# Five scheduling changes at once in a two-layer hybrid decoder: order of weight splits, table work, warm-up fillers, mixing

## The chip, the core and the metric

The kernel runs on one core of one Trainium2 chip. A core has five engines that each follow a list of instructions in order and meet at semaphores: TensorE (PE, matrix products into PSUM), VectorE (DVE), ScalarE (ACT), GpSimd (POOL) and SyncE (SP, which here only issues DMAs). The metric is the device time of one execution in microseconds. Half a per cent is about 2.5 us here.

## The reference

For 512 tokens of width 1024 the reference runs two layers, all in float32. Each layer computes

```
h = rmsnorm(x, norm_g);  p = h @ w_in        # split by columns into four head groups
A: latent attention, 4 heads: q = rmsnorm(rmsnorm(cq) @ w_uq), rotated in 32 of 96 columns;
   k from rmsnorm(ckv) @ w_ukv and one rotated key for all heads; causal softmax, times v
B: c_b * short_conv(c_c * c_h)               # width 3 along the tokens
C: sg_u * (tril(sg_w) @ layernorm(sg_v) + sg_b)   # inside chunks of 128 tokens
D: block-sparse attention on mq, mk, mv, rotated in 16 of 64 columns
x = x + concat(A*silu(g_a), B*silu(g_b), C*silu(g_c), D*silu(g_d)) @ w_out
```

## The kernel before, in words

**Tiles.** The tokens are four tiles t of 128 rows. For each, `pre_norm` (L632) forms `h` on DVE (x times the row's reciprocal norm times the gain `ng`), PE transposes it (`hT`), and ACT and DVE split it into a high part `hTh` and a low part `hTl`. A float32 product is made of three products of such parts by `mm3` (L260): high by high, high by low, low by high. Every weight is split in the same way.

**Units.** A weight block is a `Unit`: SP loads it into one of two `raw` slots, ACT (or DVE, where its planned clock is ahead) writes `whi`, DVE writes `wlo` (`split_units`, L395; for the first four units POOL writes the second low half), and PE uses both. There are six `whi`/`wlo` slots. The units stand in one list, `order`; `unit()` (L437) marks the next `AHEAD` units of the list as wanted when one is used, and an unwanted unit is only split while ACT and DVE are idle by plan.

**The planner.** Nothing of the order is left to a scheduler of the compiler. `Order` (L69) runs when the program is built: chains of work are generators with a due time and a priority, and four clocks (A, V, G, D for ACT, DVE, POOL and DMA) and `now` (PE's time) follow planned costs. Whatever chain comes next writes its instruction, and so fixes the order on its engine. All instructions of `_emit` carry L164 and those of `pe()` L194, so the profile tells them apart by tile names. If PE is idle by plan before 15 us, `pe()` writes fillers. On the chip the engines keep this order, and wait where the plan was too early.

**Around the change.** `start()` (L1548) writes the beginning: the load of the gain row `gz` on ACT's DMA queue, products of ones (`warm`), the transpose of the positions, and `ng`, a product that copies the gain row to all partitions. `rope_tables()` (L481) computes sine and cosine for the rotations with some 50 small operations on DVE, or on POOL when DVE is not free. `load_params` and `mix_chain` (L837) prepare and issue the mixing of group C: `sgw` is masked and split, the chain waits for the four tiles of `vn` (the normed `sg_v`, split into `vnh` and `vnl`), takes an `h` slot for `mix`, and writes the products `mp`. `mla_heads` (L1169) starts attention A with the transposes `t0a` of Q and `t1a` of K; it waits for all tiles of Q and K and their rotation. The output product runs as seven half-size products (`ZPROD`), whose results lie in PSUM banks of two pools (accS and sS).

**Order in each layer.** `cq` (the latent columns), then `sq` (`sg_v` and `mq`, four units), `ga`, `mp`, `kv`, attention A, the other feature columns, attention D, and the output product.

Of the kernel before, what the change touches and what calls it, by code (L numbers as in the profile page):

```python
# [18 lines left out]
P = 128  # L19
# [11 lines left out]

NRAW, NW, NT2 = 2, 6, 9
WSLACK = 0.0
AHEAD = 4
NWARM, FILL, FILLEND = 3, 0.6, 15000.0
ROPET, PAUSE, MIXT = 3900.0, (4700.0, 15500.0), 23000.0
LOPOOL = (("c0_0", 1), ("c1_0", 1), ("c2_0", 1), ("c3_0", 1))
LOPRIO = -5
ROPEB, ROPEV = 400.0, 200.0
EARLY = ('sq0', 'sq1', 'sq2')  # L40
YORDER, YCUT = (2, 3, 0, 1, 4, 6, 5, 7), 6
# [27 lines left out]
class Order:  # L69
# [20 lines left out]
    def resume(self, prio, gen):  # L90
        try:
            w = next(gen)
        except StopIteration:
            return
        if isinstance(w, Event):
            if w.t is None:
                w.waiters.append((prio, gen))
            else:
                self.spawn(gen, self.now, prio)
        else:  # L100
            self.spawn(gen, w, prio)
# [51 lines left out]
class Chain:  # L153
# [30 lines left out]
    def pe(self, cost, f, *a, **k):  # L184
        if self.t != self.pe_t:
            while self.t + PEMARGIN > self.o.now:
                yield self.t + PEMARGIN
        if self.o.now < self.o.fill_until:
            for _ in range(int((self.o.now - self.o.pe_end) * FILL / 110.0)):
                self.o.fill()  # L190
        self.o.now += cost
        self.o.pe_end = self.o.now
        self.t = self.pe_t = self.o.now + PELAT
        f(*a, **k)  # L194
# [12 lines left out]
def hybrid_trunk(ctx: ExitStack, tc: tile.TileContext, x, positions, norm_g, w_c, w_f, w_t, w_o, mla_q_norm_g,  # L207
# [27 lines left out]
    v4S = Slots(o, 4, lambda name, shape, dt: v4p.tile(shape, dt, tag="v4", name=name))  # L235
    ydS = Slots(o, 2, lambda name, shape, dt: big.tile(shape, dt, tag="yd", bufs=2, name=name))
    tkS = Slots(o, 2, lambda name, d: tkp.tile([P, NT, 4, d], F32, tag="tk", name=name))
    hS = Slots(o, 2, lambda name: wk.tile([P, D], F32, tag="h", bufs=2, name=name))
    yaS = Slots(o, 1, lambda name: wk.tile([P, S], F32, tag="ya", name=name))
    obS = Slots(o, 1, lambda name: wk.tile([P, S], F32, tag="ob", name=name))  # L240
    zzS = Slots(o, 1, lambda name: wk.tile([P, S + 2], F32, tag="zz", name=name))
# [33 lines left out]

    x1d = dr.tile([S, D], F32, name="x1d")


    class Unit:
        def __init__(self, src, a, b, name):  # L280
            self.src, self.a, self.b, self.name = src, a, b, name
            self.loaded, self.ready, self.wanted = Event(), Event(), False
            self.half, self.landed = [Event(), Event()], [Event(), Event()]
            self.slots = eS if name[:-2] in EARLY else wS

        def view(self):
            n = self.a * self.b
            return (self.hi[:, :n].rearrange("p (a b) -> p a b", a=self.a),
                    self.lo[:, :n].rearrange("p (a b) -> p a b", a=self.a))

    units, order = {}, []
    early = []

    def early_make(name):
# [100 lines left out]
    def split_units(i0, i1):  # L395
        for u in order[i0:i1]:
            ch = Chain(o)
            if u.name != "c0_0":
                yield from ch.wait(u.loaded)
            u.hi, u.lo = yield from u.slots.get(ch, u.name)  # L400
            n = u.a * u.b
            for i in range(2):
                if u.name == "c0_0":
                    yield from ch.wait(u.landed[i])
                while ch.t > o.now + SLACK:
                    yield ch.t - SLACK
                while not u.wanted and max(o.clk["A"], o.clk["V"]) > o.now + WSLACK:
                    yield o.now + 100.0
                sl = slice(i * n // 2, (i + 1) * n // 2)
                c2 = Chain(o, max(o.now, ch.t))  # L410
                hi, lo, raw = u.hi[:, sl], u.lo[:, sl], u.raw[:, sl]
                if o.clk["V"] + 600.0 < o.clk["A"] and u.idx > 3:
                    yield from c2.dve_fast(V.tensor_copy, hi, raw)
                else:
                    yield from c2.act(A.activation, hi, raw, AF.Copy)
                if u.idx < 4:
                    o.spawn(low_half(u, i, c2, lo, raw, hi), None, LOPRIO)
                    continue
                yield from c2.dve(V.tensor_tensor, lo, raw, hi.bitcast(F32), op=ALU.subtract)
            if u.idx < 4:  # L420
                continue
            ch.t = c2.t
            u.raw_slots.put(ch)
            o.set(u.ready, ch.t)

    def low_half(u, i, ch, lo, raw, hi):
        if (u.name, i) in LOPOOL:
# [8 lines left out]

    def unit(ch, name, half=None):  # L437
        u = units[name]
        for v in order[u.idx:u.idx + AHEAD]:
            v.wanted = True  # L440
        yield from ch.wait(u.ready if half is None else u.half[half])
        return u.view()
# [3 lines left out]
    def shared(slots, n):  # L446

        left = [n]

        def put(ch):  # L450
            left[0] -= 1
            if left[0] == 0:
                slots.put(ch)
        return put
# [25 lines left out]

    def rope_tables():  # L481
        ch = Chain(o)
        sc = yield from t2S.get(ch, "rope_scratch")
        def carve(i):
            return sc[:, i * 64:(i + 1) * 64].rearrange("p (t i) -> p t i", t=NT)
# [4 lines left out]

        def free_engine():

            while True:
                if ch.t > o.now + SLACK:
                    yield ch.t - SLACK
                if PAUSE[0] < o.now < PAUSE[1]:
                    yield PAUSE[1]
                if o.clk["V"] <= o.now + ROPEV:
                    return True
                if o.clk["G"] <= o.now + SLACK:  # L500
                    return False
                yield o.now + 60.0
# [90 lines left out]
    for l in range(DEPTH):  # L593
        L = Layer()
        L.l = l
        L.ng_ev = Event()
        L.hT, L.hTh = [[Event(), Event()] for _ in range(NT)], [[Event(), Event()] for _ in range(NT)]
        L.xss = [cst.tile([P, 4], F32, name=f"xss{t}_{l}") for t in range(NT)]
        L.qd = [Event() for _ in range(NT)]
        L.kd = [Event() for _ in range(NT)]  # L600
# [31 lines left out]
    def pre_norm(L, t, xx, t0, release):  # L632
# [4 lines left out]
        yield from ch.wait(L.ng_ev)  # L637
        h = yield from hS.get(ch, f"h{t}_{L.l}")
        hput = shared(hS, 2)
        tps = []  # L640
        for c in range(2):
            sl = slice(c * 512, (c + 1) * 512)
# [194 lines left out]
    def mix_chain(L):  # L837
# [11 lines left out]
        obS.put(ch)  # L849
        for t in range(NT):  # L850
            yield from ch.wait(L.vn_ev[t])
        L.mix = (yield from hS.get(ch, f"mix{l}")).rearrange("p (n g d) -> p n g d", n=NT, g=4)
        for g2 in range(2):
            mp = yield from accS.get(ch, f"mp{g2}_{l}")
# [314 lines left out]
    def mla_heads(L):  # L1169
# [2 lines left out]
            yield from ch0.wait(L.qd[t])  # L1172
            yield from ch0.wait(L.kd[t])
        yield from ch0.wait(L.kr_ev)

        def prep(H):
            H.prep_ev = [Event(), Event()]
            H.op = [None, None]
# [178 lines left out]
    def main():  # L1357
# [24 lines left out]
        def seven(L):  # L1382
# [33 lines left out]

            bank, evs = {}, {}
            home = {"b11": "z", "b21": "z", "t3": "x", "t4": "x"}
            slot = {"z0": accS, "z1": accS, "x0": accS, "x1": sS, "y0": sS, "y1": sS}
            for n in ZPROD:  # L1420
                for i in range(2):
                    b = home.get(n, "y") + str(i)
# [5 lines left out]
                    a = bank[b]  # L1428
                    if (l, n, i) == (DEPTH - 1, "b22", 1):
                        ev2 = Event()  # L1430
                        yield from z_out(L, "u", i, a, m.t, ev2, sS.put)
                        for c0, c1 in TAIL:
                            a = yield from accS.get(m, f"ot{c0}_{l}")
                            yield from prod(n, i, a, True, c0, c1)
                            o.spawn(z_out(L, n, i, a, o.now + PELAT, Event(), accS.put, c0, c1))
                        continue
                    yield from prod(n, i, a, n in ("b11", "t3"))
                    if n == "b11":
                        y = bank[f"y{i}"] = yield from sS.get(m, f"oy{i}_{l}")
                        o.spawn(minus(i, a, y, o.now + PELAT, ev))  # L1440
                    else:
                        o.spawn(z_out(L, n, i, a, o.now + PELAT, ev,
                                      slot[b].put if n in ("b21", "t4", "b22") else None))
# [102 lines left out]
    L0.x0, L0.xh = [Event() for _ in range(NT)], [Event(), Event()]  # L1546

    def start():  # L1548
        o.clk["D"] = 1000.0
        cw = Chain(o)  # L1550
        ones = (yield from zzS.get(cw, "ones"))
        gz = yield from hS.get(cw, "gz")
        nc.scalar.dma_start(gz[0:1, :], dram(norm_g, 0, [[D, 1], [1, D]]))
        yield from cw.dve_fast(V.memset, ones[:, 0:256], 1.0)
        wp = yield from accS.get(cw, "warm")
        for _ in range(NWARM):
            PE.matmul(wp[:, 0:256], ones[:, 0:P], ones[:, 0:256], start=True, stop=True)
        PE.transpose(wp[:, 256:256 + NT], junk[0:NT, P:2 * P], ident[0:NT, 0:NT])
        V.tensor_copy(posf, wp[:, 256:256 + NT])
        L0.ng = []  # L1560
        for c in range(2):
            L0.ng.append((yield from sS.get(cw, f"ng{c}")))
            PE.matmul(L0.ng[c], ones[0:1, 0:P], gz[0:1, c * 512:(c + 1) * 512], start=True, stop=True)
        o.pe_end, o.fill_until = 6300.0, FILLEND
        o.fill = lambda: PE.transpose(wp[:, 0:P], ident, ident)
        o.clk["V"] = 3700.0
        zzS.put(Chain(o, 6000.0))
        hS.put(Chain(o, 6000.0))

        def fill_end():  # L1570
            o.fill_until = 0.0
            accS.put(Chain(o))
            return
            yield
        o.spawn(fill_end(), FILLEND, -9)
        L0.ng_ev.t = 6200.0
        cg = Chain(o)
        x0 = yield from v4S.get(cg, "x0_0", [P, D], F32)
        L0.x[0] = x0
# [15 lines left out]
        o.spawn(load_units(), None, 4)  # L1595
        o.spawn(split_units(0, 4), None, LOPRIO)
        o.spawn(split_units(4, len(order)), None, 5)
        o.spawn(rope_tables(), ROPET, 6)
        o.spawn(main(), None, 10)
        for t in range(NT):  # L1600
            def pre(t):
# [64 lines left out]
```

## Time and profile before

| what | value |
|---|---|
| median of 3 runs (lowest, highest) | 498.72 us (497.2, 499.32) |
| profiled execution | 499.26 us |
| its span | 497.6 us |
| DVE, ACT, POOL busy | 384.1, 320.7, 150.6 us |
| data moved | 81.98 MB, 165 GB/s in the mean |

The span runs from the first to the last recorded instruction; the execution's own time is 1.66 us longer. The ends of PE's matrix products are modelled, so PE's busy time is an upper value, and the starts are the better measure: 512 columns take 0.227 us start to start once the clock is up. In the timelines a row has the start, the length, engine, line, operation, output and inputs, and in brackets the idle time of that engine just before, with what ended it.

### The profile page before, as it was taken

To read this page: it belongs to the slowest core of one execution; us is meant where nothing else is said; L and a number is where in the kernel's file an instruction comes from. 1 tells how busy PE (TensorE), PEld (TensorE's weight loads), DVE (VectorE), ACT (ScalarE), POOL (GpSimd) and SP (SyncE) were. 2 spreads that over 40 slices of the span, in tenths; PEclk is the share of its full clock that TensorE was granted. 3 is DMA by queue.
4 is the path that set the end of the run, shared out by engine and by line. 5 is a ranking of instruction groups with operands and counts; after the bars stand their busy time and mean duration, and the time that the engine had idled before them with its cause. 6 is when DMAs were issued, how large, how long until landed. Compare 5 with 4: busy or idle time off the path is not lost.

```text
span 497.6 us, 7823 instructions
## 1 busy us (share of the span) xinstructions
PE 490.7 (99%) x2459; PEld 416.4 (84%) x2459; DVE 384.1 (77%) x998; ACT 320.7 (64%) x938; POOL 150.6 (30%) x310
## 2 busy tenths in 40 slices
PE   8999989999999999999999999999999999999997
PEld 5998878888888888888889987788888888888886
DVE  3887885567797978699898698757888979765992
ACT  5788754557767786667566995557868676524640
POOL 4656785566100000000041478634250010000000
PEclk9999999999999999999999999999999999999999
DMA  8446549472752445587573232576259464475652
GB/s 306 110 144 212 198 100 235 147 156 54 202 139 84 149 148 135 157 315 247 165 258 129 84 125 88 193 191 102 67 191 232 150 154 122 166 258 180 229 171 96
DMA packets 35459, 81.98 MB, mean 165 GB/s; under 512 B 7125, under 2 KB 16857, under 8 KB 35162
## 3 DMA queue, kind: packets, MB, share of 16 engines
q1 hardware_dynamic: 26960, 73.09, 43.1%
q0 software_dynamic: 8448, 8.39, 11.3%
q8 instruction: 19, 0.31, 0.3%
q14 instruction: 22, 0.18, 0.1%
q10 hardware_dynamic: 10, 0.01, 0.0%
HBM read 73.61 MB, written 24.64 MB: 197 GB/s over the span
## 4 chain that ended last, share of the span: by engine, by line
PE 89%; DVE 3%; ACT 3%; POOL 3%; issue 1%; POOLq 0%; DVEq 0%
PE kv L194 10%; PE cq L194 8%; PE oy L194 6%; PE ch L194 4%; PE cc L194 4%; PE gd L194 4%; PE gb L194 4%; PE cb L194 4%; PE gc L194 4%; PE su L194 4%; PE ox L194 4%; PE oz L194 4%; PE sa L194 3%; PE ga L194 2%; PE od L194 2%; PE oa L194 2%
## 5 line engine op out<-in xcount | busy, mean ns | idle before, releaser
L164 ACT ACTIVATE pd<-pd,mnd 128x256 f32<-128x256 f32 (+3 forms) x48 | 26.0, 555 | 1.4 <-DVE mnd L164 1.4
L164 ACT ACTIVATE pha<-pTa 128x512 fp32r<-128x512 f32 (+3 forms) x32 | 13.9, 436 | 20.0 <-PE pTa L194 19.8
L194 PE MATMUL kv<-whi_kv,hTh 128*128 128x512 f32 x64 | 25.9, 405 | 0.0
L164 ACT ACTIVATE pa<-pa,mna 128x256 f32<-128x256 f32 (+3 forms) x46 | 23.9, 537 | 2.7 <-DVE mna L164 2.7
L164 ACT ACTIVATE phd<-pTd 128x512 fp32r<-128x512 f32 (+3 forms) x32 | 13.8, 434 | 17.8 <-PE pTd L194 17.8
L164 DVE TENSOR_TENSOR pla<-pTa,pha 128x512 fp32r<-128x512 f32 (+3 forms) x32 | 15.2, 484 | 12.8 <-ACT pha L164 12.7
L194 PE MATMUL kv<-whi_kv,hTl 128*128 128x512 f32 x64 | 25.0, 391 | 0.0
L194 PE MATMUL kv<-wlo_kv,hTh 128*128 128x512 f32 x64 | 24.9, 390 | 0.0
L194 PE MATMUL cq<-whi_c,hTh 128*128 128x416 f32 x64 | 24.4, 382 | 0.0
L339 POOL DMA_DIRECT2D t<-in_w_o_dram x16 | 17.5, 1097 | 19.9 <-DMA t<-t 19.3
L194 PE MATMUL cq<-whi_c,hTl 128*128 128x416 f32 x64 | 23.0, 360 | 0.0
L194 PE MATMUL cq<-wlo_c,hTh 128*128 128x416 f32 x64 | 22.9, 357 | 0.0
L164 POOL TENSOR_SCALAR xss<-xss 128x1 f32<-128x1 f32 x8 | 3.1, 391 | 61.8 <-ACT jk L164 49.1
L164 ACT ACTIVATE whi_t<-raw_t 128x512 fp32r<-128x512 f32 x31 | 18.2, 621 | 5.7 <-DMA raw_t<-t 5.7
L164 DVE TENSOR_TENSOR wlo_t<-raw_t,whi_t 128x512 fp32r<-128x512 f32 x32 | 21.1, 683 | 0.0
L164 DVE CUSTOM_DVE_ANT_0 pa<-sa,maskb 128x512 f32<-128x512 f32 (+3 forms) x32 | 15.0, 482 | 6.2 <-PE sa L194 3.1
L164 DVE CUSTOM_DVE_ANT_0 pd<-sd,maskb 128x256 f32<-128x256 f32 (+3 forms) x32 | 14.9, 485 | 5.9 <-PE pTd L194 2.8
L194 PE MATMUL sq<-yTh,hTh 128*128 128x512 f32 x48 | 18.9, 393 | 0.0
L194 PE MATMUL sq<-yTh,hTl 128*128 128x512 f32 x48 | 18.7, 390 | 0.0
L194 PE MATMUL sq<-yTl,hTh 128*128 128x512 f32 x48 | 18.7, 389 | 0.0
L164 DVE TENSOR_TENSOR pld<-pTd,phd 128x512 fp32r<-128x512 f32 (+3 forms) x32 | 15.3, 482 | 3.2 <-ACT phd L164 3.1
L164 ACT ACTIVATE whi_b<-raw_b 128x512 fp32r<-128x512 f32 x24 | 14.5, 622 | 4.2 <-DMA raw_b<-in_w_o_dram 4.2
(379 smaller groups left out, 1856.0 us busy)
## 6 DMA issues: line engine op xcount, KB each, us to landing
t<-in_w_o_dram POOLq DMA_DIRECT2D x16, 512.0 KB, 6.7
raw_t<-t SPq DMA_DIRECT2D x16, 512.0 KB, 4.2
raw_b<-in_w_o_dram SPq DMA_DIRECT2D x12, 512.0 KB, 4.4
raw_sq<-in_w_t_dram SPq DMA_DIRECT2D x8, 512.0 KB, 3.6
t<-in_w_o_dram SPq DMA_DIRECT2D x8, 512.0 KB, 4.4
raw_kv<-in_w_t_dram SPq DMA_DIRECT2D x8, 512.0 KB, 3.5
t<-t SPq DMA_DIRECT2D x8, 512.0 KB, 5.5
ys<-ysc SPq DMA_DIRECT2D x14, 256.0 KB, 4.8
```

The costliest lines, as they stand in the source:

```text
L164: f(*a, **k)
L194: f(*a, **k)
L339: nc.gpsimd.dma_start(z_src(l, n, j), quad(l, b, j), accum_op=ALU.add, max_dma_last_dim=1024)
```

## The change

- Splits: AHEAD goes from 4 to 5. A unit's split gets priority -1 while the unit is one of the next two (URGENT), and 5 otherwise. The fourth unit of `sq` is split into the two `h` slots instead of a weight slot, once the last tile's `h` has its slot.
- Tables: the first 18 operations go to DVE at once; the rest only from 30 us planned time, when DVE or POOL is free. The pause from 4.7 to 15.5 us goes.
- Fillers: products of 128 x 128 ones in place of transposes, one for 215 ns of planned idle time instead of 110. `ng` uses all 128 rows of a `gz` that DVE and POOL zero first; the load of the gain row follows the zeroing.
- Mixing: `mix_chain` goes on 2000 ns of planned time after the last `vn` is ready.
- Output product: three of the six PSUM banks come from the other pool.

```diff
-AHEAD = 4
+AHEAD = 5
-ROPET, PAUSE, MIXT = 3900.0, (4700.0, 15500.0), 23000.0
+ROPET, ROPE0, MIXT = 30000.0, 18, 23000.0
+MIXLAG = 2000.0
+URGENT, PIPE = 2, False
...
-            for _ in range(int((self.o.now - self.o.pe_end) * FILL / 110.0)):
+            for _ in range(int((self.o.now - self.o.pe_end) * FILL / 215.0)):
...
-            self.slots = eS if name[:-2] in EARLY else wS
+            self.slots = eS if name[:-2] in EARLY else HPair(int(name[-1])) if name[:-2] == "sq3" else wS
...
                 while not u.wanted and max(o.clk["A"], o.clk["V"]) > o.now + WSLACK:
                     yield o.now + 100.0
+                if u.idx > 3:
+                    yield o.now, 5 if u.idx > current[0] + URGENT else -1
...
+            done[0] += 1
+            if done[0] <= ROPE0:
+                ch.t = o.now
+                return True
+            if done[0] == ROPE0 + 1:
+                yield ROPET
             while True:
                 if ch.t > o.now + SLACK:
                     yield ch.t - SLACK
-                if PAUSE[0] < o.now < PAUSE[1]:
-                    yield PAUSE[1]
...
         for t in range(NT):
             yield from ch.wait(L.vn_ev[t])
+        yield max(o.now, ch.t) + MIXLAG
...
-            slot = {"z0": accS, "z1": accS, "x0": accS, "x1": sS, "y0": sS, "y1": sS}
+            slot = {"z0": accS, "z1": sS, "x0": sS, "x1": sS, "y0": accS, "y1": accS}
...
+        G.memset(gz[:, 512:1024], 0.0)
+        yield from cw.dve_fast(V.memset, ones[:, 0:256], 1.0)
+        yield from cw.dve_fast(V.memset, gz[:, 0:512], 0.0)
         nc.scalar.dma_start(gz[0:1, :], dram(norm_g, 0, [[D, 1], [1, D]]))
-        yield from cw.dve_fast(V.memset, ones[:, 0:256], 1.0)
         wp = yield from accS.get(cw, "warm")
-        for _ in range(NWARM):
-            PE.matmul(wp[:, 0:256], ones[:, 0:P], ones[:, 0:256], start=True, stop=True)
+        o.clk["V"] = 3000.0
+        def dense(n):
+            PE.matmul(wp[:, 0:n], ones[:, 0:P], ones[:, 0:n], start=True, stop=True)
+        dense(256)
         PE.transpose(wp[:, 256:256 + NT], junk[0:NT, P:2 * P], ident[0:NT, 0:NT])
         V.tensor_copy(posf, wp[:, 256:256 + NT])
+        for _ in range(NWARM - 1):
+            dense(256)
         L0.ng = []
         for c in range(2):
             L0.ng.append((yield from sS.get(cw, f"ng{c}")))
-            PE.matmul(L0.ng[c], ones[0:1, 0:P], gz[0:1, c * 512:(c + 1) * 512], start=True, stop=True)
+            PE.matmul(L0.ng[c], ones[:, 0:P], gz[:, c * 512:(c + 1) * 512], start=True, stop=True)
+        dense(P)
-        o.fill = lambda: PE.transpose(wp[:, 0:P], ident, ident)
+        o.fill = lambda: dense(P)
...
-        o.spawn(rope_tables(), ROPET, 6)
+        o.spawn(rope_tables(), None, -9)
```

`current[0]` is the list position of the unit last asked for, and `HPair.get` waits for the last tile's `h` and then takes both `h` slots.

More of the change, by code (lines that the diff above doesn't have):

```diff
@@ L94, in resume @@
             return
+        if isinstance(w, tuple):
+            w, prio = w
         if isinstance(w, Event):
@@ L237, in hybrid_trunk @@
     tkS = Slots(o, 2, lambda name, d: tkp.tile([P, NT, 4, d], F32, tag="tk", name=name))
-    hS = Slots(o, 2, lambda name: wk.tile([P, D], F32, tag="h", bufs=2, name=name))
+    hS = Slots(o, 2, lambda name, dt=F32: wk.tile([P, D], dt, tag="h", bufs=2, name=name))
     yaS = Slots(o, 1, lambda name: wk.tile([P, S], F32, tag="ya", name=name))
@@ L276, in hybrid_trunk, with __init__, get, put @@
     x1d = dr.tile([S, D], F32, name="x1d")
+    class HPair:
+        def __init__(self, l):
+            self.l = l
+        def get(self, ch, name):
+            yield from ch.wait(layers[self.l].h_got)
+            w = []
+            for x in ("hi", "lo"):
+                w.append((yield from hS.get(ch, f"w{x}_{name}", F32R)))
+            return w
+        def put(self, ch):
+            hS.put(ch)
+            hS.put(ch)
     class Unit:
@@ L289, in view @@
                     self.lo[:, :n].rearrange("p (a b) -> p a b", a=self.a))
-    units, order = {}, []
+    units, order, current = {}, [], [0]
     early = []
@@ L415, in split_units @@
                     yield from c2.act(A.activation, hi, raw, AF.Copy)
[L416 to L424, printed above, removed]
+                low = low_half(u, i, c2, lo, raw, hi)
+                if u.idx < 4 or PIPE:
+                    o.spawn(low, None, LOPRIO if u.idx < 4 else 5 if u.idx > current[0] + URGENT else -1)
+                else:
+                    yield from low
     def low_half(u, i, ch, lo, raw, hi):
@@ L438, in unit @@
         u = units[name]
+        current[0] = u.idx
         for v in order[u.idx:u.idx + AHEAD]:
@@ L482, in rope_tables @@
         ch = Chain(o)
+        done = [0]
         sc = yield from t2S.get(ch, "rope_scratch")
@@ L597, in hybrid_trunk @@
         L.hT, L.hTh = [[Event(), Event()] for _ in range(NT)], [[Event(), Event()] for _ in range(NT)]
+        L.h_got = Event()
         L.xss = [cst.tile([P, 4], F32, name=f"xss{t}_{l}") for t in range(NT)]
@@ L639, in pre_norm @@
         hput = shared(hS, 2)
+        if t == L.torder[-1]:
+            o.set(L.h_got, o.now)
         tps = []
@@ L1430, in seven @@
                         ev2 = Event()
-                        yield from z_out(L, "u", i, a, m.t, ev2, sS.put)
+                        yield from z_out(L, "u", i, a, m.t, ev2, slot[b].put)
                         for c0, c1 in TAIL:
@@ L1438, in seven @@
                     if n == "b11":
-                        y = bank[f"y{i}"] = yield from sS.get(m, f"oy{i}_{l}")
+                        y = bank[f"y{i}"] = yield from slot[f"y{i}"].get(m, f"oy{i}_{l}")
                         o.spawn(minus(i, a, y, o.now + PELAT, ev))
@@ L1548, in start @@
     def start():
-        o.clk["D"] = 1000.0
+        o.clk["D"] = 1500.0
         cw = Chain(o)
@@ L1562, in start @@
             L0.ng.append((yield from sS.get(cw, f"ng{c}")))
-            PE.matmul(L0.ng[c], ones[0:1, 0:P], gz[0:1, c * 512:(c + 1) * 512], start=True, stop=True)
-        o.pe_end, o.fill_until = 6300.0, FILLEND
-        o.fill = lambda: PE.transpose(wp[:, 0:P], ident, ident)
-        o.clk["V"] = 3700.0
-        zzS.put(Chain(o, 6000.0))
-        hS.put(Chain(o, 6000.0))
+            PE.matmul(L0.ng[c], ones[:, 0:P], gz[:, c * 512:(c + 1) * 512], start=True, stop=True)
+        dense(P)
+        o.pe_end, o.fill_until = 7200.0, FILLEND
+        o.fill = lambda: dense(P)
+        hS.put(Chain(o, 7200.0))
         def fill_end():
@@ L1572, in fill_end @@
             accS.put(Chain(o))
+            zzS.put(Chain(o))
             return
@@ L1575, in start @@
         o.spawn(fill_end(), FILLEND, -9)
-        L0.ng_ev.t = 6200.0
+        L0.ng_ev.t = 6500.0
         cg = Chain(o)
```

## The prediction

> **What bounds the kernel now.** I read the page first: the span, the busy shares and the shares of the chain.
>
> ```profile
> span 497.6 us, 7823 instructions
> ...
> PE 490.7 (99%) x2459; PEld 416.4 (84%) x2459; DVE 384.1 (77%) x998; ACT 320.7 (64%) x938; POOL 150.6 (30%) x310
> ...
> PE 89%; DVE 3%; ACT 3%; POOL 3%; issue 1%; POOLq 0%; DVEq 0%
> ```
>
> PE is busy 99% of the span and 89% of the chain, so an edit gains only where PE stands still or does work that goes away. The profiled execution took 499.26 us, 1.66 more than its span; the median of the runs shown is 498.72. The sum below starts from 499.26.
>
> Next comes the windows view, for where PE stands still. After the window come its length and PE busy, then PEld, DVE, ACT and POOL, with instruction counts in brackets.
>
> ```profile
> 60.00:70.00 10.00, 9.53 (x43) 7.55 (x41) 8.15 (x31) 4.76 (x20) 8.95 (x16) 1.00 0.28 66
> 70.00:80.00 10.00, 9.05 (x44) 7.56 (x45) 7.86 (x24) 5.09 (x12) 8.47 (x10) 1.00 1.02 204
> 80.00:310.00 230.00, 230.00 (x1167) 196.41 (x1166) 184.88 (x485) 155.57 (x457) 63.20 (x132) 1.00 0.52 159
> 310.00:320.00 10.00, 9.12 (x45) 7.32 (x44) 6.92 (x21) 5.49 (x15) 6.24 (x18) 1.00 0.56 210
> ```
>
> From 80 to 310 PE is full. The two short places are the mixing products `mp` of each layer; the timeline of PE shows them.
>
> ```profile
> 69.14 0.39 PE L194 MATMUL ga<-hTh,wlo_ga 128*128 128x512 f32 x1
> 70.85 0.38 PE L194 MATMUL mp<-vnh,wsh 128*128 128x256 f32 x1 [1.31 <-ACT vnh L164]
> 71.33 0.39 PE L194 MATMUL mp<-vnl,wsh 128*128 128x256 f32 x1
> 71.56 0.28 PE L194 MATMUL mp<-vnh,wsl 128*128 128x256 f32 x1
> 71.67 0.28 PE L194 MATMUL mp<-vnh,wsh 128*128 128x256 f32 x1
> ...
> 305.01 0.39 PE L194 MATMUL sq<-whi_sq,hTl 128*128 128x512 f32 x1
> 305.24 0.39 PE L194 MATMUL ga<-hTh,whi_ga 128*128 128x512 f32 x1
> ...
> 310.45 0.39 PE L194 MATMUL ga<-hTh,wlo_ga 128*128 128x512 f32 x1
> 311.62 0.39 PE L194 MATMUL mp<-vnh,wsh 128*128 128x256 f32 x1 [0.78 <-ACT vnh L164]
> 312.10 0.39 PE L194 MATMUL mp<-vnl,wsh 128*128 128x256 f32 x1
> ```
>
> A 512-column product takes 0.23 us start to start (305.01 to 305.24), a 256-column one 0.11 (71.56 to 71.67). From 69.14 to 71.33 are 2.19 us for 0.34 of work: 1.85 lost. From 310.45 to 312.10, 1.65 for 0.34: 1.31 lost. Both wait for `vnh`, then `vnl`, of the last token tile: 3.16 us in all. Beside the start, nothing else here is there to be won.
>
> **The change part by part.**
>
> *MIXLAG, the mixing products two planned microseconds later.* I compared the order of instructions on each engine in both programs. In layer 0 PE now has 33 more 512-column products ahead of `mp` (24 `ga1`, 9 `kv0`), 33 x 0.227 = 7.5 us, so it arrives at 69.37 + 7.5 = 76.9. DVE has more ahead of `vnl` as well.
>
> ```profile
> 66.95 0.42 DVE L164 BATCH_NORM_STATS2 bst<-sq 128x6 f32<-128x256 f32 x1
> ...
> 70.86 0.42 DVE L164 TENSOR_TENSOR vnl<-vn,vnh 128x256 fp32r<-128x256 f32 x1
> 72.22 0.48 DVE L164 SCALAR_TENSOR_TENSOR mq<-mq,mmq,dq_b 128x64 f32<-128x64 f32 x2 [0.94 <-POOL mmq L164]
> ...
> 73.48 0.68 DVE L164 SCALAR_TENSOR_TENSOR th_ga<-th_ga,ga 128x512 f32<-128x512 f32 x1
> 74.08 1.29 DVE L164 TENSOR_TENSOR wlo_kv<-raw_kv,whi_kv 128x512 fp32r<-128x512 f32 x2
> ...
> 79.69 0.36 DVE L164 SCALAR_TENSOR_TENSOR rope_scratch<-rope_scratch 128x64 f32<-128x64 f32 x2
> ```
>
> New ahead of the last `vnl`: a memset (0.3), 23 table operations (0.36 for two that overlap, 0.15 each start to start: 3.4), six of the Q rotation (0.8), four `mq` (0.8), one `th_ga` (0.6) and four `wlo_kv` halves (2.4): some 8.5 us. The first `mq` of the last tile, which waited for POOL's `mmq` until 72.22, now stands ahead of `vnl`, with 3.9 us of work between. That is a new wait in front of `vnl`. `mmq` came 5.3 us after `bst` (66.95); with `bst` as now or 1 us later, `vnl` ends at 76.1 to 77.1, against PE's 76.9. I charge 0.2 us. The bounds are 0 and, if none of the 8.5 us falls into idle time, 71.28 + 8.5 - 76.9 = 2.9.
>
> In layer 1 `mp` comes 12 `ga` products later (2.7 us) and the old distance from `bst` to the end of `vnl` (307.67 to 312.05, next fence) holds, so its wait goes: `vnl` ends 6.8 us after `sq`, PE arrives after 8.2.
>
> *Table work in DVE's idle beginning.* The tables are ready some 20 us sooner, because 18 operations stand at DVE's front. PE was full between 80 and 310, so that alone is worth 0. But the planner now issues attention sooner: layer 1's first transposes `t0a` come right behind `mp0`. Their last input is the rotated Q, behind this chain:
>
> ```profile
> 307.67 0.42 DVE L164 BATCH_NORM_STATS2 bst<-sq 128x6 f32<-128x256 f32 x1
> ...
> 311.63 0.42 DVE L164 TENSOR_TENSOR vnl<-vn,vnh 128x256 fp32r<-128x256 f32 x1
> ...
> 318.04 0.35 DVE L164 TENSOR_TENSOR Q<-Q,rbq 128x64 f32<-128x64 f32 x2
> ...
> 311.85 1.07 POOL L164 TENSOR_TENSOR mmq<-mmq,nhalf 128x4 f32<-128x4 f32 x1
> ...
> 320.35 0.60 PE L194 MATMUL t0a<-ident,Q 128*96 128x128 f32 x4
> ```
>
> Before, Q is ready at 318.39 and used at 320.35. After the change the last Q operation stands 2.8 us of DVE work behind the first `mq` that needs `mmq`. `sq` ended at 305.24, `bst` began 2.4 later (DVE was behind), `mmq` ended 5.25 after that (312.92). So Q is ready 2.4 + 5.25 + 2.8 = 10.5 us after `sq`. PE reaches `t0a` after the old 5.4 (305.24 to 310.68), 12 `ga` (2.7) and six `mp` (0.7): 8.9. Wait: **1.6 us**. The bounds: 0, if DVE reaches `bst` at once (10.5 - 2.4 is under 8.9); and 1.6 + 4.7 = 6.3, if nothing is absorbed of the 4.7 us that DVE has more ahead of this place than before (two `wlo_kv` halves at 0.6 and three hi copies at 0.4 near it, the rest far earlier). I take 1.6, since the lag of 2.4 is the row's own. In layer 0 attention moves up by some 10 us of PE work, but there the Q rotation moves up too and by the same sums is ready 3 us ahead: 0.
>
> *Start: dense fillers and a zeroed gain tile.*
>
> The timelines of ACT, POOL, PE and DVE, one behind the other:
>
> ```profile
> 1.40 0.23 ACTq L1553 DMA_DIRECT2D gz<-in_norm_g_dram  x1
> 1.66 1.28 ACT L164 ACT_TABLE_LOAD   x1 [1.66 <-PEq L1651]
> 3.52 0.60 ACT L164 ACTIVATE sq<-x 128x512 f32<-128x512 f32 x1 [0.57 <-DMA x<-in_x_dram]
> 4.05 0.19 ACT L164 ACTIVATION_READ_ACCUMULATOR sq<-x 128x1 f32 x1
> 4.60 0.60 ACT L164 ACTIVATE sq<-x 128x512 f32<-128x512 f32 x1 [0.36 <-DMA x<-in_x_dram]
> ...
> 1.38 0.52 POOL L467 MEMSET maskb<- 128x512 f32 x1
> ...
> 2.46 0.58 POOL L478 MEMSET inv<- 128x1 f32 x16
> ...
> 12.58 4.00 POOL L164 TENSOR_TENSOR wlo_c<-raw_c,whi_c 128x416 fp32r<-128x416 f32 x3 [0.37 <-ACT whi_c L164]
> ...
> 4.24 3.76 PE L1563 MATMUL ng<-gz,ones 1*128 1x512 f32 x4
> ...
> 12.92 0.55 PE L194 MATMUL cq<-whi_c,hTl 128*128 128x416 f32 x1
> ...
> 14.26 0.35 PE L194 MATMUL cq<-wlo_c,hTh 128*128 128x416 f32 x1
> ...
> 8.04 0.75 DVE L164 SCALAR_TENSOR_TENSOR h<-x,xss,ng 128x512 f32<-128x512 f32 x1 [0.47 <-PE ng L1563]
> ```
>
> The `gz` load was issued at 1.40. In the changed program it waits for the two memsets that zero `gz` and for a DMA semaphore that x's second half must raise first. The memset on POOL stands behind the 16 of `inv` (to 3.04) and ends near 3.6 (0.52 for 512 columns, as `maskb`); x's half lands at about 4.5, since the `sq` at 4.60 waited for it. It stands in ACT's queue ahead of the table load (1.28) and the squares, so these wait too: the first `sq` moves from 3.52 to about 6.1, and `ng` begins between 6 and 7.3 (at most 2.8 us lay between issue and use). I take 6.5; it ends 3.76 later, near 10.2, where `h` had it at 8.04. First transposes and `cq` come about 1.6 us later. Against that stands work that goes: 12 transposes as fillers (0.21 each, cold) for five dense products. The last of the three POOL halves `wlo_c` (16.58) moves by 0.6 to 1.7 us with ACT's copies. I charge **+0.5**; the upper end is +1.5 (all of POOL's delay shows), the lower -0.9 (the rival below).
>
> *AHEAD 5, URGENT, sq3 in the `h` slots, swapped PSUM banks, k and MoBA rotations on DVE.* They move splits between idle places of ACT and DVE, PE does the same products, and SP issues the same 189 loads and stores in nearly the same order. I cost them at 0: from 80 to 310 DVE is busy 184.88 of 230, which is the cover. Gone, the price is a split half each (0.6 to 0.7).
>
> **Sum:** 499.26 - 1.85 - 1.31 + 0.2 + 1.6 + 0.5 = **498.4 us**, no change against 498.72.
>
> **The rivals.**
>
> *Clock and DVE both better.* Transposes and one-row `ng` ran from 4.24 to 10.6 and PE was still slow at 12.92 (0.55) and fast at 14.26 (0.35), some 3.3 us after `cq` began at 10.6. If the 128-row `ng` counts as `cq` did, the clock is up near 10: six `cq` (0.16 each) and eight transposes (0.1) save 1.8, less the 0.9 that 1.6 us of delay are worth at half speed. The start is then -0.9, and if DVE keeps up, `t0a` doesn't wait: 498.4 - 1.4 - 1.6 = **495.4**. The Trainium skill says so ("TensorE: Matmul & The Clock Gate", Part 1 and Part 4): the clock comes up after a sustained window of about 3.4 us, which runs free, and transposes don't count as busy. The rows agree on both; no run yet shows `ng` with 128 rows. Against it: ng's start waits, and c1 to c3 arrive later.
>
> *Slower: DVE never catches up.* Place: Q at `t0a` of layer 1. DVE was busy 6.92 of 10 from 310 to 320 and 7.86 to 8.15 around the other `mp`, so for it speaks the density, against it the idle fifth. Price 6.3 instead of 1.6: **503.1**. The kernel is slower than 501.2 from a wait of 4.4 on, which is DVE reaching `bst` 5.2 us after `sq`.
>
> *The change doesn't do what it says.* The wait at `mp` of layer 0 stays, as `vnl` moved back with it: 2.9 instead of 0.2, **501.1**.
>
> **How the numbers follow.** Half a per cent, about what a measurement of this kernel can tell from no change, is 2.5 us: 496.2 to 501.2. Forecast 0.45 (its own range 496.8 to 500.5); better clock and DVE 0.23; DVE never catches up 0.17; wait stays 0.15. Faster: 0.20 of the second and 0.02 of the first. Slower: 0.17 and 0.03 of the last. That leaves 0.58 for the same. The range reaches from 495.2 to 502.2: below it is the best of the second case, above it the worst of the third.
>
> **What would show it.** In the profile after, right: 10.00 PE busy in both windows around `mp`, a PE wait of 1 to 2 us at `t0a` of layer 1 for DVE's Q, the first `sq` near 6 us behind the table load. Wrong: `sq` still at 3.5; `mp` waiting for `vnl`; a `cq` of 0.35 before 12; a wait for `whi` or `wlo` of a weight split anywhere after 20 us.

## The result: slower by 1.35 per cent

The changed kernel takes 505.37 us in the median (504.17 to 506.83, 6 runs) against 498.87 for the kernel before (497.2 to 499.32, 6 runs). The ratio is 1.0135, 95% interval 1.0112 to 1.0157. The forecast was 498.4 with a range to 502.2, which is 7 us too low.

The page of the profile after, first the span, then the busy shares and the chain. The profiled execution took 506.0 us.

```profile
span 504.3 us, 7817 instructions
...
PE 490.9 (97%) x2457; PEld 415.7 (82%) x2457; DVE 388.1 (77%) x1019; ACT 319.8 (63%) x939; POOL 143.3 (28%) x288
...
PE 81%; POOL 6%; ACT 4%; DMA 4%; DVE 3%; issue 1%; SPq 0%; POOLq 0%; ACTq 0%; DVEq 0%
```

PE's busy time is the same (490.9 after 490.7), and its share of the chain has gone from 89% to 81%. So most of the loss is PE waiting, with POOL, ACT and a DMA in the chain where PE was. The view of waits for PE names them (total, times, longest):

```profile
PE ng L1599 <- DMA gz<-in_norm_g_dram: 4.3, 1, 4.3
PE t0a L198 <- DVE Q L168: 2.0, 1, 2.0
PE cT L198 <- DVE hTl L168: 1.6, 1, 1.6
PE warm L1590 <- DVE ones L168: 1.3, 1, 1.3
PE kv L198 <- ACT mix L168: 0.5, 1, 0.5
```

`warm` is no news (1.3 before as well). `hTl`, which `cT` (the transposes of the latent columns) waits for, is made by DVE out of ACT's `hTh`. There is no row for `mp`, which now begins at 82.32 and 317.71:

```profile
82.32 0.28 PE L198 MATMUL mp<-vnh,wsh 128*128 128x256 f32 x1
```

The windows that were short before are full now (in the first two only because `mp` has moved out of them), and others are short. The column behind POOL is the granted clock:

```profile
60.00:70.00 10.00, 10.00 (x45) 8.20 (x44) 9.24 (x34) 6.79 (x31) 8.90 (x16) 1.00 0.46 160
70.00:80.00 10.00, 10.00 (x46) 8.27 (x45) 8.67 (x30) 5.59 (x17) 9.59 (x15) 1.00 0.76 165
...
310.00:320.00 10.00, 8.69 (x42) 7.10 (x40) 8.06 (x27) 5.32 (x17) 7.42 (x14) 1.00 0.33 105
320.00:330.00 10.00, 9.33 (x44) 8.25 (x45) 5.36 (x17) 5.88 (x14) 1.85 (x6) 0.83 0.47 159
```

**Where the 6.7 us of span came from.** Three instructions of PE have the same work before them in both programs, fillers aside: the first `cT` (20.49 before, 23.98 after), the first `ga` of layer 0 (63.93, 69.37) and the first `ga` of layer 1 (305.24, 309.53). So the loss is 3.5 us at `cT`, 5.4 at layer 0's `ga`, 4.3 at layer 1's `ga` and 6.7 at the end. The start costs 3.5; the wait at the second `cT` 1.7 more; then 1.85 at `mp` is won and 0.7 at `kv` lost; in layer 1, 1.3 at `mp` is won and 2.1 at `t0a` lost. The last 1.7 is the clock. The waits in this sum are read from start to start, less the normal pitch of the products, and so lie a little above the idle times of the view. Together 3.5 + 1.7 - 1.85 + 0.7 - 1.3 + 2.1 + 1.7 = 6.6.

**The start.** The timelines of ACT, PE and DVE after:

```profile
4.51 0.23 ACTq L1584 DMA_DIRECT2D gz<-in_norm_g_dram  x1
4.77 1.28 ACT L168 ACT_TABLE_LOAD   x1 [4.77 <-DVE rope_scratch L168]
6.06 0.60 ACT L168 ACTIVATE sq<-x 128x512 f32<-128x512 f32 x1
...
9.44 3.78 PE L1599 MATMUL ng<-gz,ones 128*128 128x512 f32 x4 [4.29 <-DMA gz<-in_norm_g_dram]
...
14.94 0.45 PE L198 MATMUL cq<-whi_c,hTh 128*128 128x416 f32 x1
...
13.26 0.75 DVE L168 SCALAR_TENSOR_TENSOR h<-x,xss,ng 128x512 f32<-128x512 f32 x1 [0.88 <-PE ng L1599]
```

The gain row's load is issued at 4.51, where the forecast put it, and the table load and the squares stand behind it as foreseen. (The memsets were done at 3.5; ACT's queue then stood at the semaphore of x's second load, raised last at 4.41.) But its 4 KB are there only at 9.40, 4.9 us after issue. Before, issue was at 1.40 and the load's semaphore was raised at 3.26, 1.9 us later; `ng` at 4.24 wasn't waiting for it any more. What lies between is traffic: after 2.5 us the loads of x and of the first weights fill the DMA engines (their share is 1.00 to 1.04 from 5 to 13 us), and x's own tiles took 8.0 us to land (median). The gain row runs on ACT's queue, q10, and not on that of the big loads, q1. The DMA view from 4.5 to 8.7 us, then from 8.7 to 9.1:

```profile
q1 hardware_dynamic: 567, 1.55, 102.5%
...
q10 hardware_dynamic: 2, 0.00, 2.6%
```

Up to 8.7 us only packets of q1 have run. The gain row's one packet starts at 8.72, 4.2 us after the issue, and takes 0.16 us. Before it started 1.2 us after the issue. So it is waiting and not moving that takes the time.

**Attention and the clock.** PE at `t0a` of layer 1, then the granted clock in windows of 1 us:

```profile
318.42 0.27 PE L198 MATMUL t0a<-ident,Q 128*96 128x128 f32 x1
320.67 0.55 PE L198 MATMUL t0a<-ident,Q 128*96 128x128 f32 x3 [1.98 <-DVE Q L168]
...
323.58 0.63 PE L198 MATMUL ga<-hTl,whi_ga 128*128 128x512 f32 x1
```

```profile
320.00:321.00 1.00, 0.33 (x3) 0.33 (x4) 0.61 (x3) 0.00 (x0) 0.24 (x2) 1.00 1.48 492
321.00:322.00 1.00, 1.00 (x7) 0.97 (x6) 0.12 (x1) 0.59 (x1) 0.92 (x6) 0.53 0.08 33
322.00:323.00 1.00, 1.00 (x7) 1.00 (x6) 1.00 (x2) 0.89 (x2) 0.69 (x1) 0.50 0.01 0
323.00:324.00 1.00, 1.00 (x4) 0.82 (x4) 1.00 (x4) 0.67 (x3) 0.00 (x0) 0.50 0.00 0
324.00:325.00 1.00, 1.00 (x5) 0.80 (x4) 0.04 (x1) 0.75 (x2) 0.00 (x0) 0.77 0.53 172
```

PE waits from 318.7 to 320.7 for the rotated Q. Then the granted clock is at half for some 3.4 us: 0.47 + 0.50 + 0.50 + 0.23 = 1.7 us of work not done. A busy PE (1.00) hides this; only the clock column and the matmul of 0.63 instead of 0.39 us show it.

**ACT held up by a split.** ACT and PE, first near the second `cT`, then near `kv` (`yTh` is the slot of `sq`'s high half here):

```profile
32.77 0.63 ACT L168 ACTIVATE yTh<-raw_sq 128x512 fp32r<-128x512 f32 x1 [3.59 <-DMA raw_sq<-in_w_t_dram]
33.31 0.58 ACT L168 ACTIVATE hTh<-hT 128x512 fp32r<-128x512 f32 x1
33.78 0.62 ACT L168 ACTIVATE yTh<-raw_sq 128x512 fp32r<-128x512 f32 x1
34.30 0.59 ACT L168 ACTIVATE hTh<-hT 128x512 fp32r<-128x512 f32 x1
...
34.78 0.55 PE L198 MATMUL cT<-ident,ct 128*128 128x128 f32 x3 [1.56 <-DVE hTl L168]
...
86.86 0.63 ACT L168 ACTIVATE whi_gc<-raw_gc 128x512 fp32r<-128x512 f32 x1 [3.16 <-DMA raw_gc<-in_w_f_dram]
87.39 0.82 ACT L168 ACTIVATE mix<-mp,sgb 128x256 f32<-128x256 f32 x2
...
87.90 0.50 PE L198 MATMUL kv<-whi_kv,hTh 128*128 128x512 f32 x1 [0.55 <-ACT mix L168]
```

ACT stands idle for 3.6 and 3.2 us at the copy of a weight whose load hasn't landed. Behind it stand `hTh`, which PE's next step needs, and `mix`, which empties PE's bank. ACT is idle there, and yet it sets the time. How much depends on the execution: see experiment 5.

### The profile page after: what moved, and what is told of

Read it like the earlier page. It is cut to its first block, busy times and chain, and to the rows that moved or that the text cites. A ratio compares the mean times of both kernels' runs of the same rounds, so it can differ in the third digit from the quotient of the medians.

```text
span 504.3 us, 7817 instructions
## 1 busy us (share of the span) xinstructions
PE 490.9 (97%) x2457; PEld 415.7 (82%) x2457; DVE 388.1 (77%) x1019; ACT 319.8 (63%) x939; POOL 143.3 (28%) x288
## 4 chain that ended last, share of the span: by engine, by line
PE 81%; POOL 6%; ACT 4%; DMA 4%; DVE 3%; issue 1%; SPq 0%; POOLq 0%; ACTq 0%; DVEq 0%
PE kv L198 9%; PE oy L198 6%; PE cq L198 5%; PE cc L198 4%; PE cb L198 4%; PE gd L198 4%; PE ch L198 4%; PE gb L198 4%; PE gc L198 4%; PE su L198 4%; PE ox L198 4%; PE oz L198 4%; PE sa L198 3%; ACT junk L168 2%; PE sq L198 2%; POOL mmq L168 2%
## 5 line engine op out<-in xcount | busy, mean ns | idle before, releaser
L168 ACT ACTIVATE pa<-pa,mna 128x256 f32<-128x256 f32 (+3 forms) x48 | 25.2, 537 | 1.5 <-DVE mna L168 1.4
L168 ACT ACTIVATE hTh<-hT 128x512 fp32r<-128x512 f32 x16 | 9.4, 595 | 13.6 <-PE hT L198 13.6
L168 DVE CUSTOM_DVE_ANT_0 pd<-sd,maskb 128x384 f32<-128x384 f32 (+3 forms) x32 | 15.0, 484 | 1.8 <-PE pTd L198 1.4
```

## The experiments

Each ran beside the kernel before, whose median there was 498.7 to 499.0 us; the ratios are to that.

**1. The gain row early,** on the changed kernel. Every other instruction keeps its place on its engine.

```diff
-        G.memset(gz[:, 512:1024], 0.0)
+        nc.scalar.dma_start(gz[0:1, :], dram(norm_g, 0, [[D, 1], [1, D]]))
         yield from cw.dve_fast(V.memset, ones[:, 0:256], 1.0)
-        yield from cw.dve_fast(V.memset, gz[:, 0:512], 0.0)
-        nc.scalar.dma_start(gz[0:1, :], dram(norm_g, 0, [[D, 1], [1, D]]))
...
-            PE.matmul(L0.ng[c], ones[:, 0:P], gz[:, c * 512:(c + 1) * 512], start=True, stop=True)
+            PE.matmul(L0.ng[c], ones[0:1, 0:P], gz[0:1, c * 512:(c + 1) * 512], start=True, stop=True)
```

> The changed kernel, with the gain row loaded at the very start again: neither memset of gz, ng a product of one row. Every other instruction keeps its place in its engine's list. Theory (the late gain row costs the start): the table load runs at about 1.7 us instead of 4.8, ng begins near 4.3 instead of 9.4, the first cq near 11 instead of 14.9, and the time falls by about 4 us from 505.4 to about 501.4; if the later wait at 34.8 us (1.7 us, for a weight load) is a consequence of the late start, to about 499.7. Rival (the start is made good later, the loss is that of the split order alone): 504 to 505.

Measured: 500.73 us (499.55 to 502.35), ratio to before 1.0056 (1.0038 to 1.0075), 4.6 us less than the changed kernel. `cT` begins at 20.45, as in the kernel before. So the late load is nearly the whole loss of the start, and none of it is made good later. A rest is hidden in this execution: the first `cq` still comes at 11.47 instead of 10.62, and the clock came up sooner (products of 0.35 us from 12.78 on, before from 14.26). The wait at the second `cT` (now near 31 us) is still 1.3, so it isn't a consequence of the start, and the one at `kv` is 1.3 (0.7 in the changed kernel).

**2. The mixing later, alone,** on the kernel before.

```diff
+        yield max(o.now, ch.t) + 2000.0
         L.mix = (yield from hS.get(ch, f"mix{l}")).rearrange("p (n g d) -> p n g d", n=NT, g=4)
```

> The kernel before with one part of the change, the mixing issued 2000 ns of planned time later. PE has 2.1 us more work ahead of mp in both layers. Theory (mp then comes after its vnl and nothing else moves): PE's waits of 1.85 and 1.31 us go, time 498.9 - 3.2 = 495.7. Rival (the wait moves on to the next user of the PSUM bank or to attention): 498 to 499.

Measured: 496.39 us, ratio 0.9948 (0.9931 to 0.9965). The waits for `vnh` and `vnl` are gone; 0.85 us in layer 0 and 0.3 in layer 1 came back at the second `mp`, which waits for its PSUM bank until DVE has done `th_ga`; PE's timeline:

```profile
73.21 0.39 PE L194 MATMUL mp<-vnh,wsh 128*128 128x256 f32 x1 [0.71 <-DVE th_ga L164]
```

**3. The zeroed gain tile, alone,** on the kernel before.

```diff
+        G.memset(gz[:, 512:1024], 0.0)
+        yield from cw.dve_fast(V.memset, ones[:, 0:256], 1.0)
+        yield from cw.dve_fast(V.memset, gz[:, 0:512], 0.0)
         nc.scalar.dma_start(gz[0:1, :], dram(norm_g, 0, [[D, 1], [1, D]]))
-        yield from cw.dve_fast(V.memset, ones[:, 0:256], 1.0)
...
-            PE.matmul(L0.ng[c], ones[0:1, 0:P], gz[0:1, c * 512:(c + 1) * 512], start=True, stop=True)
+            PE.matmul(L0.ng[c], ones[:, 0:P], gz[:, c * 512:(c + 1) * 512], start=True, stop=True)
```

> The kernel before with one part of the change, gz zeroed by two memsets and then loaded, and ng over 128 rows; all other instructions keep their place. Theory: the load of the gain row is issued at about 4.5 instead of 1.4 and lands near 9.4, first cq 4 us later, time 498.9 + 3 to 4 = 502 to 503. Rival 1 (128 rows lift the clock early and pay for the delay): 499. Rival 2 (the loss came from the dense fillers and table work, not from the gain row): 498.9.

Measured: 503.46 us, ratio 1.0098 (1.0083 to 1.0113), 4.7 us more than before. PE's timeline:

```profile
10.09 3.49 PE L1565 MATMUL ng<-gz,ones 128*128 128x512 f32 x4 [5.71 <-DMA gz<-in_norm_g_dram]
```

Issue at 4.42, `ng` at 10.09; no other instruction has changed its place. With the first experiment the cause is shown from both sides.

**4. No urgent splits,** on top of experiment 1.

```diff
-                    yield o.now, 5 if u.idx > current[0] + URGENT else -1
+                    yield o.now, 5
```

> The changed kernel with the gain row loaded early (as in the first experiment, 500.7 us), and every later split at priority 5 instead of -1 for the next two units. The plan shifts with it: in layer 1 t0a now stands 5.5 us of PE work further behind sq. Theory (splits put first stand in ACT's queue before their load has landed and hold up the hTh and mix copies behind them: 1.3 us at cT near 31, 1.3 us at kv near 84): both waits go, and the 1.85 us at t0a with them, 500.7 - 4.4 = 496.3. Rival (the loads are late for another reason and PE waits for the splits themselves instead): 499.5 to 501.

Measured: 500.55 us, ratio 1.0047 (1.0031 to 1.0064): no gain over 500.73. The two waits behind ACT's split copies are gone, as the theory had it. But the new order has waits of its own, as PE's view of waits shows:

```profile
PE t0a L198 <- POOL Q L168: 1.0, 1, 1.0
PE sa L198 <- DVE lo1a L168: 0.7, 1, 0.7
PE mp L198 <- DVE vnl L168: 0.6, 1, 0.6
```

The rival was right on the time. That PE waits for the splits themselves was not: none of these waits is for a `whi` or `wlo`.

**5. Attention held,** with the gain row early as well (the expectation leaves that edit out; compare with experiment 1).

```diff
         yield from ch0.wait(L.kr_ev)
+        yield max(o.now, ch0.t) + 3000.0
```

> The changed kernel, with the first attention's chain held for 3000 ns of planned time in both layers, so that in layer 1 PE has 6.9 us of other products more between mp and t0a. Theory (t0a came too early for the rotated Q, 2.1 us, and the pause took the clock down, 1.8 us): the wait at t0a of layer 1 goes and the granted clock stays at 1.00 there; time 505.4 - 3.9 = 501.5. Rival (DVE is the bound there and the wait moves to the next product that needs it): 504.5 to 505.5.

Measured: 498.05 us, ratio 0.9987 (0.9978 to 0.9997), 2.7 us less than experiment 1. There is no wait at `t0a`. The waits at `cT` and `kv` are 0.6 and 0.4 here, against 1.3 and 1.3 in experiment 1, but the hold can't have done that: up to 87 us every engine has the same instructions in the same order in both. The same holds for the changed kernel (1.7 and 0.7) and experiment 9 (0.7 and 1.4). So these two waits, which hang on when a weight's load lands, vary by about 1 us from execution to execution, and part of the 2.7 may be that.

**6. Dense fillers, alone,** on the kernel before.

```diff
-            for _ in range(int((self.o.now - self.o.pe_end) * FILL / 110.0)):
+            for _ in range(int((self.o.now - self.o.pe_end) * FILL / 215.0)):
...
-        o.fill = lambda: PE.transpose(wp[:, 0:P], ident, ident)
+        o.fill = lambda: PE.matmul(wp[:, 0:P], ones[:, 0:P], ones[:, 0:P], start=True, stop=True)
...
-        zzS.put(Chain(o, 6000.0))
...
+            zzS.put(Chain(o))
```

(The last two lines keep the tile of ones until the fillers end.)

> The kernel before with one part of the change, the fillers: products of ones in place of transposes, one per 215 ns of planned idle time; the gain row, ng and the rest keep their place. Theory (transposes don't bring the clock up, products do): fast products from about 12.4 us instead of 13.9, 0.5 to 1 us less, 498.8 - 0.8 = 498.0. Rival (the clock counts only the long cq products): no change, 498.8.

Measured: 499.16 us, ratio 1.0004 (0.9990 to 1.0019): nothing. The rival's time was right, and its reason isn't shown: in this execution the clock was up from about 4 us (`ng` took 2.01 us from 4.24, before 3.76) and fell again at about 7.8, while PE waited 1.6 us for `h`. The windows, with the granted clock behind POOL (the column also reads 1.00 ahead of the first change of the clock that is recorded, as in the kernel before at 12 us, where a `cq` takes 0.55 us; there the length of the products tells):

```profile
6.00:7.00 1.00, 0.89 (x5) 0.52 (x4) 0.00 (x0) 0.41 (x1) 0.21 (x1) 1.00 0.99 323
7.00:8.00 1.00, 0.00 (x0) 0.00 (x0) 0.83 (x2) 0.68 (x2) 0.24 (x1) 0.88 1.02 366
8.00:10.00 2.00, 1.52 (x7) 1.53 (x8) 1.08 (x2) 1.10 (x3) 0.82 (x1) 0.50 1.02 400
```

**7. Mixing later and dense fillers.** Experiments 2 and 6 together.

> The kernel before with two parts of the change, the mixing 2000 ns later (alone 496.4 us) and the dense fillers. Theory (the two are independent): 496.4 - 0.8 = 495.6. Rival (the earlier start is lost again in a later wait): 496.4.

Measured: 497.3 us, ratio 0.9975 (0.9963 to 0.9987), 0.9 us above experiment 2's 496.39. The fillers win nothing here either.

**8. Tables alone,** on the kernel before: 18 operations at once, the rest from 30 us, no pause, priority -9, as in the change's diff.

> The kernel before with one part of the change, 18 table operations at once on DVE and the rest from 30 us of planned time. Layer 0's attention comes 16.5 us of PE work sooner and mp 1.4 us later; layer 1 keeps its order. Theory (tables alone cost nothing, they only let attention move): half of the wait at mp of layer 0 goes, 498.8 - 0.9 = 497.9, and no wait at t0a of layer 1. Rival (attention before its inputs is what tables bring): a new wait of 1 to 3 us at t0a of layer 0, 499 to 501.

Measured: 503.93 us, ratio 1.0107 (1.0081 to 1.0133). Neither figure was right; the rival's wait at `t0a` of layer 0 is there (1.2 us), and the first `cq` comes at 12.75 instead of 10.62. The positions come at 4.42 as in the kernel before, so the 18 operations hold up `h` in DVE's timeline:

```profile
8.18 1.52 DVE L164 SCALAR_TENSOR_TENSOR rope_scratch<-rope_scratch 128x64 f32<-128x64 f32 x6
9.62 0.58 DVE L164 TENSOR_TENSOR wlo_c<-raw_c,whi_c 128x416 fp32r<-128x416 f32 x1
10.12 1.40 DVE L164 SCALAR_TENSOR_TENSOR h<-x,xss,ng 128x512 f32<-128x512 f32 x2
```

The change takes the positions first (2.86 us). With the gain row early (experiment 1) DVE is done with the 18 operations at 7.3, and the second half of `h` waits for `ng` (to 9.00), so there they cost no start. In layer 1 tables alone leave `t0a` where it was in the order.

**9. Attention held, late gain row kept.** The edit of experiment 5 on the changed kernel.

> The changed kernel as it is, late gain row included, with the first attention's chain held for 3000 ns of planned time; the order is that of the kernel that had both edits (498.05 us), but for the memsets. Theory (attention too early costs its wait of 2.1 us, the clock's fall behind it 1.8 us and some of the waits before): 505.4 - 3.9 = 501.5 or a little below, and the granted clock is 1.00 in layer 1. Rival (the fall of the clock comes from the late start and not from the pause): the clock falls again somewhere in layer 1, 503 to 503.5. The difference from 498.05 prices the late gain row without the clock's fall: 3.5 by the theory.

Measured: 501.92 us, ratio 1.005 (1.0032 to 1.0068), 3.5 us less than the changed kernel. The granted clock is 1.00 in all four runs, so the rival, by which the late start takes the clock down, was wrong. The late gain row is worth 501.92 - 498.05 = 3.9 here.

**10 and 11. Mixing later by 2500 and by 3000 ns,** alone, on the kernel before.

> The kernel before with the mixing 2500 ns later instead of 2000 (alone 496.4 us, with 0.85 us left at mp of layer 0 and 0.3 in layer 1, where the second mp waits for its PSUM bank until DVE has done th_ga). PE has 0.7 us more work ahead of mp. Theory: the rest of the wait goes, 495.5. Rival (the bank is freed later in turn, or t0a of layer 1, which comes 2.1 us sooner, waits): 496.4 or more.

> The kernel before with the mixing 3000 ns later: 1.3 us more of PE work ahead of mp than with 2000. Theory: no wait at mp, 495.4. Rival (kv or attention then waits for the bank, or t0a for Q): 496 to 497.5.

Measured: 495.38 us, ratio 0.9925 (0.9908 to 0.9941), and 495.34 us, ratio 0.9927 (0.9912 to 0.9943). Both beat both kernels, by 3.6 us against before. With 3000 PE's view of waits holds only the first memset:

```profile
PE warm L1558 <- DVE ones L164: 1.3, 1, 1.3
```

**12. The order of splits, alone,** on the kernel before.

```diff
-AHEAD = 4
+AHEAD = 5
+URGENT = 2
...
+                if u.idx > 3:
+                    yield o.now, 5 if u.idx > current[0] + URGENT else -1
```

> The kernel before with one part of the change, the order of the splits (AHEAD 5 and priority -1 for the next two units). In the written order mp of layer 0 comes 3.4 us of PE work later, mp of layer 1 0.7 later, and t0a of layer 1 4.7 us sooner, as far behind sq (8.9 us) as in the changed kernel, though the tables are as before. Theory (it is the order of the splits, not the tables, that brings attention forward and blocks ACT): PE waits about 1.9 us at t0a of layer 1 for Q and 1 to 2.6 us behind ACT's split copies, less 2.5 us at mp: 498.8 - 2.5 + 3 to 4.5 = 499.3 to 500.8. Rival (ACT's blocking came from the late or cold start and is gone here): 498.2 or less.

Measured: 502.86 us (500.17 to 503.81), ratio 1.0062 (1.0038 to 1.0087). More than expected, and at other places: no wait at `t0a`, since `mp` before it waits 1.8 us and gives Q the time. But PE's view of waits, taken in the slowest of the seven runs (503.81), has 2.4 and 1.5 us in the output product (`oy`, `oz`) and 1.4 at attention D's `pTd`:

```profile
PE oy L197 <- DVE xr L167: 2.4, 1, 2.4
PE oz L197 <- DVE yD L167: 1.5, 1, 1.5
PE pTd L197 <- DVE mq1d L167: 1.4, 1, 1.4
```

The changed kernel has none of these three. It also has the other PSUM banks for the output product, which was not tried alone. What the run does show is the order: these splits, with the old tables, put `t0a` 8.9 us of PE work behind `sq`, as in the changed kernel. Tables alone did not, and without the urgent splits (experiment 4) `t0a` goes 5.5 us further back.

## Why the prediction was wrong, step by step

- **Mixing later, -3.16 + 0.2: right.** Both waits went (no PE wait at `mp`, 82.32 and 317.71, in the changed kernel; experiments 10 and 11 on their own, and experiment 2 but for a rest of 0.85 and 0.3). The rival in which the wait stays was wrong.
- **Wait at `t0a` of layer 1, +1.6: right in place and cause of the wait, 2.1 in size.** The chain from `sq` through `mmq` to Q was as worked out; its terms were 1.6, 6.5 and 3.0 us in place of 2.4, 5.25 and 2.8, and PE came after 8.9, as forecast. The step blamed the tables for moving `t0a`; the written orders of experiments 8 and 12 show that the splits' order moved it.
- **The start, +0.5, at most +1.5: this failed.** It measured +3.5 in the profile, and 3.9 to 4.7 in the runs. Issue at 4.5 and the queue behind it were right. The term that was mis-sized is the load's own time, taken as 2 (at most 2.8) from a load issued at 1.40, with the DMA engines at a share of 0.09 from 1 to 2 us; that load took 1.9. The moved one met full engines and took 4.9, of which it waited 4.2 for its packet to start. The 2.9 us more turn the +0.5 into 3.4. No row showed this load under traffic, and that should have opened the upper bound: x's whole tiles took 6.4 us to land before, by the table of DMA issues.
- **Split order at 0: this failed too,** by 1.7 + 0.7 in the profile (0.6 to 1.7 and 0.4 to 1.4 in the four traces with this order). The cover that was named, idle time on ACT and DVE, doesn't help where the split's copy waits for its load: ACT, which keeps its order, then idles (3.6 and 3.2 us), and what stands behind it is late. The sign of being wrong that was named, a wait for `whi` or `wlo`, didn't come either: PE waits for `hTl` and `mix` behind the copy. The condition that would have shown it, load against copy at each split moved forward, was not worked out.
- **The clock after a pause: not in the sum.** 1.7 us behind the wait at `t0a`.
- **Together** the misses are 3.0 at the start, 2.4 at the splits, 1.7 for the clock, 0.5 at `t0a` and -0.2 at `mp`: 498.4 + 7.4 = 505.8, against 506.0 in the profiled execution.
- **The faster rival** (128-row `ng` lifts the clock near 10) was wrong on the time: `ng` itself began at 9.4. That 128 rows lift the clock was right (last section). **The slower rival** had the place right and the price too high (6.3); the time came out 2.3 us above its 503.1 by other causes.

Open: AHEAD, the PSUM banks and `sq3` in the `h` slots were not run alone.

## What to carry to other kernels

A small load can wait behind the traffic of all queues at the time of its issue: moved by 3 us into the stretch where the big loads run, the gain row took 4.9 us instead of 1.9, and everything stood behind it. Work put first on an in-order engine must have its input by then; ask of each such step what stands behind it if its load is late. The bundle of five changes cost 6.5 us, while one of them alone (the mixing, at 2500 to 3000 ns) was worth 3.6: run the parts one by one.

## What the runs showed of the hardware

- **A pause of PE can cost more than itself.** The changed kernel had a mean granted clock of 0.997 in all six runs. The kernel of experiment 1, whose pause at `t0a` was 1.85 us, had it in two of seven executions, and these two took 502.35 and 501.90 us, the other five 499.55 to 501.42. Experiment 4, with a pause of some 1.1 us there, had it in one of nine (502.35, the others 499.66 to 501.19). With attention held (experiments 5 and 9) none of fourteen had it. The profile shows the fall behind the pause in the changed kernel; for the other executions only the mean is known, which a clock that falls again at the start (experiment 6) lowers too. A low mean alone is no loss: of 56 executions of the kernel before beside the experiments, the 13 with a mean of 0.996 or 0.997 took 497.0 to 498.3 us and the others 498.1 to 500.0. What length of pause is enough stays open.
- **When the clock comes up at the start varies from run to run with the same PE work.** With the fillers as before, products were fast from about 12.2 us in experiment 11 and from about 14 in the profiled execution of the kernel before. PE in experiment 11:

```profile
9.90 1.06 PE L194 MATMUL hT<-ident,h 128*128 128x128 f32 x4
10.62 0.69 PE L194 MATMUL cq<-whi_c,hTh 128*128 128x416 f32 x1
...
12.21 0.36 PE L194 MATMUL cq<-whi_c,hTh 128*128 128x416 f32 x1
```

This spread fits the free-running window of the Trainium skill ("TensorE: Matmul & The Clock Gate", Part 1). Its Part 4 says that transposes don't count as busy in the same way. Here the clock came up 1.6 us after the first `cq`, behind transposes from 7.93 on, so either the transposes counted in part or less than 3.4 us of products was enough; no run separates the two. Dense fillers in their place changed nothing (experiment 6).
- **Here products of 128 rows brought the clock up, products of a single row did not.** Behind each `ng` stand four transposes; first the kernel before (one row), then experiment 3 (128 rows, after PE had stood idle for 5.7 us):

```profile
7.93 1.11 PE L1565 MATMUL warm<-ident 128*128 128x128 f32 x4
...
13.41 0.60 PE L1567 MATMUL warm<-ident 128*128 128x128 f32 x4
```

The same work takes 1.11 us and 0.60 us. In the kernel before products were fast only some 3.3 us after the first `cq`.
